# GpSimd instead of VectorE for eleven subtractions in each of two feed forwards

## The chip, the cores and the metric

The kernel is one program on one core of a Trainium2 chip. The metric is the device time of one execution in microseconds (us); less is better. The core has a matmul engine (TensorE, called PE in the profile, with its weight loads in a row of their own, PEld), three engines for elementwise work (VectorE or DVE, ScalarE or ACT, GpSimd or POOL) and a queue engine (SyncE or SP) that issues transfers. Each engine works through its own list of instructions in order and waits on semaphores for the others.

## The reference

The reference is one block of a transformer with 512 tokens of width 1024, all in float32:

```python
x = x + 0.5 * swiglu(rmsnorm(x, ffn1_norm), ffn1_w_gate, ffn1_w_up, ffn1_w_down)
x = x + token_mixer(rmsnorm(x, mix_norm), ...)      # differential and dilated attention
x = x + 0.5 * swiglu(rmsnorm(x, ffn2_norm), ffn2_w_gate, ffn2_w_up, ffn2_w_down)
return rmsnorm(x, final_norm)
# GpSimd instead of VectorE for eleven subtractions in each of two feed forwards
```

The change lies in the two feed forwards (the lines with `swiglu`).

## The kernel before

**Products in three parts.** The matmuls take operands in a rounded float32 format (`F32R`). To keep precision each operand is split: a high part, which is a rounded copy that ScalarE makes (`A.copy`), and a low part, value minus high part, which until now VectorE makes. A product is then high*high, high*low, low*high: the three matmuls of `mm3` (L157 uses the weight's high part with the moving operand's high part, L158 the moving operand's low part, L159 the weight's low part).

**Layout.** The activations lie transposed: eight tiles `x[0]` to `x[7]` of 128 features by 512 tokens. A weight arrives by a transfer into `raw`, ScalarE casts it to `w` (L148, or L436 for the later units), and VectorE makes its low part (L149, or L440).

**The order of a feed forward** (`ffn`, suffix `a` for the first and `b` for the second). Of the 22 column blocks of the gate and up matrices the first ones are plain: block j multiplies all eight x tiles in two halves of four. The blocks before `n0` (5 in the first feed forward, 3 in the second) use the x tiles before the norm is known, and VectorE scales the result (L265, L268, L269). While blocks `n0-2` and `n0-1` run on TensorE, `normed_x` makes the normed tiles: VectorE writes `nx` (L280), ScalarE the high part `xh` (L282), and the low part `xl` is L283. Block `n0` is the first that reads `xh` and `xl`. After it come units of seven products (Strassen's scheme for a 2x2 split of the matrices): they need sums and differences of the normed tiles (`t_sums`, L300 and L303, which overwrite `nx`), of which `t_casts` makes high parts (`tx`, L308) and `t_rests` low parts (`tt`: L317 for three of the four pairs of tiles, L320 for the fourth). In `t_rests(p, i)`, i = 0 gives the terms t1 and t3, i = 1 the terms t4 and t2, which the units read later.

**Sums of weights.** A unit also needs sums of weight blocks. SP loads one block into `s1` and `s3` (L378) and a transfer issued by POOL adds the second one (L379). These transfers are nearly all that POOL does.

**What sets the order.** Up to block `n0` the order on VectorE, ScalarE, SP and POOL is chosen by the framework's scheduler, which weighs each instruction by its place in the source and when its inputs are due. From block `n0` on (`schedule`, with the table `FIRST` for the sums) it is the order in which the source emits them, by due times written in nanoseconds. TensorE's order is always that of the source.

Of the kernel before, what the change touches and what calls it, by code (L numbers as in the profile page):

```python
# [14 lines left out]
F32 = mybir.dt.float32  # L15
# [3 lines left out]
ALU = mybir.AluOpType  # L19
# [63 lines left out]
def tile_macaron(ctx: ExitStack, tc, xs, xT, wf, wgu1, wst1, wd1, wdg1, wqk, wv, wo, wgu2, wst2, wd2,  # L83
                 wdg2, lams, relb, onehot, addc, out):
    nc = tc.nc
    V, A, G, T = nc.vector, nc.scalar, nc.gpsimd, nc.tensor
# [10 lines left out]
    def slot(i, nm, dt=F32):  # L97
        return sl.tile([P, S], dt, tag=f"slot{i}", name=nm)


    def flat(a):
        return a.rearrange("p (b a) -> p b a", b=2)

    def evens(a):
        return a.rearrange("p (a b) -> p b a", b=2)
# [7 lines left out]
    def side(a, i):  # L113
        return a.rearrange("p (b h a) -> p h b a", b=2, h=2)[:, i]
# [6 lines left out]
    xh = [cp.tile([P, S], F32R, tag=f"xh{k}", name=f"xh{k}") for k in range(KD)]  # L121
    xl = [cp.tile([P, S], F32R, tag=f"xl{k}", name=f"xl{k}") for k in range(KD)]
# [38 lines left out]
    def gain(norm, k):  # L161
        return sm[:, norm * KD + k:norm * KD + k + 1]
# [70 lines left out]
    def ffn(wgu, wst, wd, wdg, n0, n1, norm, early, res, nm, hooks, ended, first=None,  # L233
# [13 lines left out]
        nx, th, tl, held_parts = [], [], [], {}  # L247
# [27 lines left out]
        def normed_x(p):  # L275

            for k in (2 * p, 2 * p + 1):
                n = slot(8 + k, f"nx{nm}{k}")
                nx.append(n)
                V.scalar_tensor_tensor(flat(n[:]), evens(x[k]), gain(norm, k), evens(res["bc"][:]),  # L280
                                       op0=ALU.mult, op1=ALU.mult)
                A.copy(xh[k][:], n[:])  # L282
                V.tensor_tensor(xl[k][:], n[:], xh[k][:].bitcast(F32), op=ALU.subtract)  # L283

        def t_places():
            rows = [tp.tile([P, 5 * HS], F32R, tag=f"pr{p % 2}", name=f"tt{nm}{p}")
# [26 lines left out]
        def t_rests(p, i):  # L313
            t = nx[2 * p + i]
            if p < 3:
                c = slice(i * S, (i + 1) * S)
                V.tensor_tensor(tl[p][:, c], t[:], th[p][:, c].bitcast(F32), op=ALU.subtract)  # L317
            else:
                for q in range(2):
                    V.tensor_tensor(flat(tl[p][:, i * S + q * HS:i * S + (q + 1) * HS]),  # L320
                                    side(t[:], q),
                                    flat(th[p][2 * i + q]).bitcast(F32), op=ALU.subtract)
# [340 lines left out]
        def schedule():  # L663
# [43 lines left out]
            for i, (f, *v) in enumerate(FIRST):  # L707
                f = {"sums": t_sums, "casts": t_casts, "rests": t_rests, "part": lambda j, i: held_parts[n0 + j][i]()}[f]
                at(*v[:2], f, *v[2:])

        j0 = 0
        if first is not None:
            j0 = 2
            due += first

        prepare = {(n0 - 2 + p // 2, 1 + p % 2 * 4): (normed_x, p) for p in range(4)}

        def prepared(j, k):
# [7 lines left out]
        for j in range(j0, n1):  # L726
# [12 lines left out]
            for hf in range(2):  # L739
# [4 lines left out]
                for kk in range(4):  # L744
                    k = hf * 4 + kk
# [34 lines left out]
    with tc.manual_schedule(engines={mybir.EngineType.DVE, mybir.EngineType.Activation}):  # L780
        for t in range(4):
            raw = wp.tile([P, 1024], F32, tag="raw", name=f"raw_f{t}")
            h, l = w_place()
            for kk in range(2):
                k = 2 * t + kk
# [708 lines left out]
    for i, m in enumerate((WO + 1, WO + 3)):  # L1494
        a11, a12, a21, a22 = [wo[m + j // 2][:, j % 2 * 512:j % 2 * 512 + 512] for j in range(4)]
        for j, n, parts in ((0, "s3", (a11, a21)), (1, "s2", (a21, a22, a11)),
                            (2, "s1", (a21, a22)), (3, "s4", (a21, a22, a11, a12))):
            t = sums[m, n] = slot((32, 8)[i] + j, f"{n}wo{m}")
# [151 lines left out]
    for i, (m, (o, _, _)) in enumerate(seq):  # L1650
        if i > 3:
            t = max(start[i // 2 * 2 - 4] if i > 5 else 5.2, start[i] - 4.1)
# [4 lines left out]
        if o in ("a22", "s4"):  # L1657
            k, t = m + (o == "a22"), start[i + 1]
# [4 lines left out]
    with tc.manual_schedule(engines={mybir.EngineType.DVE, mybir.EngineType.Activation}):  # L1663
        while evs:
            e = min(evs, key=lambda e: e[:2])
# [210 lines left out]
```

## Time and profile before

| what | value |
| --- | --- |
| median of 3 runs | 896.49 us (896.14 to 896.87) |
| the profiled execution | 896.77 us, span in the trace 895.0 us |
| TensorE busy | 879.5 us of the span, 98% |
| VectorE busy | 766.7 us, 86%, 1603 instructions |
| ScalarE busy | 559.6 us, 63% |
| GpSimd busy | 111.6 us, 12%, 140 instructions |
| granted TensorE clock | 0.995 |

A row of a timeline reads: start in us, length in us, engine, line and operation, output<-inputs, shapes; in brackets the idle time of the engine before it and what ended that. A row of a group reads: line, engine, operation, count | busy us, mean ns of one | idle us before them. A recorded length is from the start to the end of one instruction; on VectorE neighbours overlap a little, so what an instruction costs its engine is the distance from one start to the next. The time of the profiled execution is the span and 1.8 us around it.

### The profile page before, as it was taken

What the parts mean: (1) busy time and instruction counts of PE and PEld (TensorE: products, weight loads), DVE (VectorE), ACT (ScalarE), POOL (GpSimd) and SP (SyncE); (2) the same over time, 40 slices, a digit from 0 to 9 for tenths busy, and PEclk for the clock granted to TensorE, in tenths of its full rate; (3) what the DMA queues carried; (4) which work ended last, traced back from release to release, by engine and by line L of the source; (5) the groups of instructions that cost most, each with busy time, mean ns of one, the idle gap of its engine ahead of it and who ended that gap; (6) DMA issues with size and microseconds to landing.
All of it is one profiled execution on the core that took longest, in us unless ns stands there. A gap on an engine that the chain in (4) does not pass through costs nothing.

```text
span 895.0 us, 17681 instructions
## 1 busy us (share of the span) xinstructions
PE 879.5 (98%) x6561; PEld 835.5 (93%) x6561; DVE 766.7 (86%) x1603; ACT 559.6 (63%) x1152; POOL 111.6 (12%) x140
## 2 busy tenths in 40 slices
PE   9999999999999999999999999999999999999996
PEld 7879999999999999998989889889999999999995
DVE  7799998787998995688998859999899778799897
ACT  7457775455776673666766858557677454667563
POOL 0001200112203100001010220001110111220100
PEclk9999999999999999999999999999999999999998
DMA  7447756678857843345365674646884857985842
GB/s 262 138 136 167 181 144 179 153 192 210 208 148 209 224 137 95 118 118 157 104 173 157 172 146 118 176 134 161 188 199 116 200 166 177 235 213 124 202 130 94
DMA packets 66374, 146.86 MB, mean 164 GB/s; under 512 B 7680, under 2 KB 9984, under 8 KB 66288
## 3 DMA queue, kind: packets, MB, share of 16 engines
q1 hardware_dynamic: 48672, 113.29, 39.2%
q0 software_dynamic: 17616, 32.45, 22.3%
q8 instruction: 51, 0.84, 0.4%
q14 instruction: 35, 0.29, 0.1%
HBM read 137.28 MB, written 2.14 MB: 156 GB/s over the span
## 4 chain that ended last, share of the span: by engine, by line
PE 74%; DVE 16%; ACT 5%; issue 3%; DMA 2%; SPq 0%; POOL 0%; DVEq 0%; ACTq 0%; POOLq 0%
DVE w L939 1%; DVE pr L1222 1%; PE po L1260 1%; DVE w L440 1%; PE pdb L157 1%; PE pdb L158 1%; PE pdb L159 1%; PE pda L158 1%; PE pda L157 1%; PE pda L159 1%; PE pxub L159 1%; PE pwgb L157 1%; PE pyub L159 1%; PE pwub L159 1%; PE pygb L159 1%
## 5 line engine op out<-in xcount | busy, mean ns | idle before, releaser
L1225 ACT ACTIVATE pr<-pr,small 128x128 f32<-128x128 f32 (+3 forms) x64 | 35.7, 559 | 30.3 <-DVE small L1222 30.0
L436 ACT CAST w<-s2b 128x512 fp32r<-128x512 f32 x52 | 32.6, 626 | 22.5 <-DVE s2b L418 21.8
L436 ACT CAST w<-s2a 128x512 fp32r<-128x512 f32 x48 | 29.9, 624 | 22.6 <-DVE s2a L418 18.9
L440 DVE TENSOR_TENSOR w<-s2b,w 128x512 fp32r<-128x512 f32 x52 | 36.0, 693 | 1.2 <-ACT w L436 1.1
L1222 DVE CUSTOM_DVE_ANT_0 pr<-sc,strip 128x128 f32<-128x128 f32 (+3 forms) x64 | 29.7, 487 | 8.1 <-PE sc L1221 8.0
L1005 PE MATMUL pv<-w,xh 128*128 128x256 f32 x128 | 35.7, 279 | 0.0
L1007 PE MATMUL pv<-w,xh 128*128 128x256 f32 x128 | 35.1, 274 | 0.0
L1006 PE MATMUL pv<-w,xl 128*128 128x256 f32 x128 | 35.1, 274 | 0.0
L440 DVE TENSOR_TENSOR w<-s2a,w 128x512 fp32r<-128x512 f32 x48 | 33.1, 690 | 0.8 <-ACT w L436 0.6
L939 DVE TENSOR_TENSOR w<-raw_qk,w 128x512 fp32r<-128x512 f32 x32 | 21.7, 688 | 5.3 <-ACT w L935 5.2
L157 PE MATMUL pq<-xh,w 128*128 128x512 f32 x64 | 26.0, 407 | 0.0
L157 PE MATMUL pk<-xh,w 128*128 128x512 f32 x64 | 24.3, 380 | 0.6 <-DVE ob L1285 0.6
L1006 PEld LDWEIGHTS pv<-w,xl 128*128 128x128 f32 x128 | 24.5, 191 | 0.1
L1005 PEld LDWEIGHTS pv<-w,xh 128*128 128x128 f32 x128 | 24.5, 191 | 0.1
L1007 PEld LDWEIGHTS pv<-w,xh 128*128 128x128 f32 x128 | 24.5, 191 | 0.0
L158 PE MATMUL pk<-xl,w 128*128 128x512 f32 x64 | 24.3, 379 | 0.0
L159 PE MATMUL pk<-xh,w 128*128 128x512 f32 x64 | 24.3, 379 | 0.0
L159 PE MATMUL pq<-xh,w 128*128 128x512 f32 x64 | 24.3, 379 | 0.0
L158 PE MATMUL pq<-xl,w 128*128 128x512 f32 x64 | 24.3, 379 | 0.0
L935 ACT CAST w<-raw_qk 128x512 fp32r<-128x512 f32 x32 | 19.3, 617 | 6.7 <-PE pv L1006 3.0
L1260 PEld LDWEIGHTS po<-v,ptb 128*128 128x128 f32 x160 | 21.5, 191 | 1.8 <-ACT ptb L1249 0.8
L1260 PE MATMUL po<-v,ptb 128*128 128x128 f32 (+1 forms) x160 | 22.1, 273 | 0.2 <-ACT ptb L1249 0.2
(841 smaller groups left out, 4135.1 us busy)
## 6 DMA issues: line engine op xcount, KB each, us to landing
raw_qk<-wqk_dram SPq DMA_DIRECT2D x16, 512.0 KB, 4.0
raw0bg<-wst_dram SPq DMA_DIRECT2D x9, 512.0 KB, 5.4
raw0bu<-wst_dram SPq DMA_DIRECT2D x9, 512.0 KB, 5.9
raw_gua<-wgu_dram SPq DMA_DIRECT2D x8, 512.0 KB, 3.4
raw0ag<-wst_dram SPq DMA_DIRECT2D x8, 512.0 KB, 5.2
raw0au<-wst_dram SPq DMA_DIRECT2D x8, 512.0 KB, 5.2
raw0ad<-wdg_dram SPq DMA_DIRECT2D x8, 512.0 KB, 6.0
strip<-bias_rows SPq DMA_DIRECT2D x16, 256.0 KB, 5.2
```

What stands on the lines that cost most here:

```text
L157: T.matmul(po, wh, mh, start=first, stop=False, skip_group_check=on)
L158: T.matmul(po, wh, ml, start=False, stop=False, skip_group_check=on)
L159: T.matmul(po, wl, mh, start=False, stop=last, skip_group_check=on)
L436: A.copy(made[t][0], source(t))
L440: V.tensor_tensor(l, source(t), h.bitcast(F32), op=ALU.subtract)
L939: V.tensor_tensor(l[:, c:c + 512], raw[:, c:c + 512], h[:, c:c + 512].bitcast(F32), op=ALU.subtract)
L1005: T.matmul(po, xh[k][:, xs], mh_, start=k == 0, stop=False)
L1006: T.matmul(po, xl[k][:, xs], mh_, start=False, stop=False)
L1007: T.matmul(po, xh[k][:, xs], ml_, start=False, stop=k == KD - 1)
L1222: V.tensor_tensor_reduce(out=o, in0=a, in1=b, op0=ALU.add, op1=ALU.min, scale=1.0, scalar=3.0e38, accum_out=st["mx"][:, m, i:i + 1])
L1225: A.activation(pi, pi, AF.Exp, scale=-1.0, bias=st["mx"][:, m, i:i + 1], accum_out=st["ls"][:, m, i:i + 1])
L1260: T.matmul(st["po3"][:, i, d0:d0 + dn], st["ptb", m, i][:, k * P:(k + 1) * P], vk, start=k == 0, stop=k == i)
```

## The change

Eleven subtractions of a feed forward are written for GpSimd in place of VectorE: the eight of `normed_x` (the low parts `xl`) and, in `t_rests`, those with i = 1 for the three pairs p < 3. Those with i = 0 and the fourth pair stay on VectorE. Both feed forwards call the same function, so 22 instructions move.

```diff
@@ normed_x
                 A.copy(xh[k][:], n[:])
-                V.tensor_tensor(xl[k][:], n[:], xh[k][:].bitcast(F32), op=ALU.subtract)
+                G.tensor_tensor(xl[k][:], n[:], xh[k][:].bitcast(F32), op=ALU.subtract)
@@ t_rests
             if p < 3:
                 c = slice(i * S, (i + 1) * S)
-                V.tensor_tensor(tl[p][:, c], t[:], th[p][:, c].bitcast(F32), op=ALU.subtract)
+                e = G if i else V
+                e.tensor_tensor(tl[p][:, c], t[:], th[p][:, c].bitcast(F32), op=ALU.subtract)
```

The added line moves all later line numbers by one (L317 becomes L318, L379 becomes L380, L440 becomes L441).

**GpSimd, first feed forward.** Its list in the changed kernel, from the second transfer of the first weight sums on (the tiles carry a running number behind their name; `xl_86` to `xl_93` are the eight low parts, `nxa` and `xh` their inputs; the rows of `xl_88` to `xl_91` read like their neighbours and are left out):

```order
L380 DMA s3ag_574<-wst_dram 128x512
L283 TENSOR_TENSOR xl_86<-nxa_457,xh_78 128x512
L283 TENSOR_TENSOR xl_87<-nxa_461,xh_79 128x512
L283 TENSOR_TENSOR xl_92<-nxa_583,xh_84 128x512
L283 TENSOR_TENSOR xl_93<-nxa_587,xh_85 128x512
L380 DMA s1au_652<-wst_dram 128x512
L380 DMA s3au_655<-wst_dram 128x512
L380 DMA s1ag_733<-wst_dram 128x512
L380 DMA s3ag_736<-wst_dram 128x512
L318 TENSOR_TENSOR tta_635<-nxa_461,txa 128x512
L318 TENSOR_TENSOR tta_636<-nxa_497,txa 128x512
L318 TENSOR_TENSOR tta_637<-nxa_545,txa 128x512
```

Before, the transfers stood there alone; now the eight subtractions stand ahead of those of the second unit (`s1au_652`), and the three others ahead of `s1au_865`. The second feed forward has the same pattern.

**VectorE, blocks 3 and 4 of the first feed forward.** Before, where `raw_gua_0_525` and `raw_gua_1_561` are the weights of the two halves of block 4:

```order
L280 SCALAR_TENSOR_TENSOR nxa_497<-x_99,x_104,rbc_n_379 128x512
L283 TENSOR_TENSOR xl_87<-nxa_461,xh_79 128x512
L283 TENSOR_TENSOR xl_88<-nxa_493,xh_80 128x512
L283 TENSOR_TENSOR xl_89<-nxa_497,xh_81 128x512
L149 TENSOR_TENSOR w<-raw_gua_0_525,w 128x1024
L280 SCALAR_TENSOR_TENSOR nxa_541<-x_100,x_104,rbc_n_379 128x512
L265 TENSOR_TENSOR t1a_513<-pga_439,rbc_n_379 128x512
L268 TENSOR_TENSOR t2a_516<-pua_440,rbc_n_379 128x512
L280 SCALAR_TENSOR_TENSOR nxa_545<-x_101,x_104,rbc_n_379 128x512
```

and now:

```order
L280 SCALAR_TENSOR_TENSOR nxa_497<-x_99,x_104,rbc_n_379 128x512
L149 TENSOR_TENSOR w<-raw_gua_0_525,w 128x1024
L280 SCALAR_TENSOR_TENSOR nxa_541<-x_100,x_104,rbc_n_379 128x512
L280 SCALAR_TENSOR_TENSOR nxa_545<-x_101,x_104,rbc_n_379 128x512
L149 TENSOR_TENSOR w<-raw_gua_1_561,w 128x1024
L265 TENSOR_TENSOR t1a_513<-pga_439,rbc_n_379 128x512
L280 SCALAR_TENSOR_TENSOR nxa_583<-x_102,x_104,rbc_n_379 128x512
L268 TENSOR_TENSOR t2a_516<-pua_440,rbc_n_379 128x512
```

The low part of the first half's weight follows the third `nxa` directly, and that of the second half has moved ahead of the scaling of block 3's result (L265 to L269). Further on, the scaling of block 4's result has moved behind the first sums.

**VectorE, the first unit of seven products.** Before:

```order
L440 TENSOR_TENSOR w<-s3ag_574,w 128x512
L317 TENSOR_TENSOR tta_635<-nxa_461,txa 128x512
L317 TENSOR_TENSOR tta_636<-nxa_497,txa 128x512
L440 TENSOR_TENSOR w<-s3au_655,w 128x512
L317 TENSOR_TENSOR tta_637<-nxa_545,txa 128x512
L418 TENSOR_TENSOR s2a_786<-s1au_652,raw0au 128x512
```

and now:

```order
L441 TENSOR_TENSOR w<-s3ag_574,w 128x512
L441 TENSOR_TENSOR w<-s3au_655,w 128x512
L419 TENSOR_TENSOR s2a_786<-s1au_652,raw0au 128x512
```

Only the three subtractions have left; nothing else has moved there. TensorE's list and SP's are the same as before, and ScalarE has the same instructions with some casts of `xh` moved ahead of a weight cast.

## The prediction

> **What bounds the kernel now.** The page's first rows give TensorE 98% of the span. So time can only be won where TensorE waits. I read its waits in the two stretches that the change touches, 28 to 100 us and 560 to 650 us; each list has one row (line waited at, what ended the wait, total us, times, longest).
>
> ```profile
> PE 879.5 (98%) x6561; PEld 835.5 (93%) x6561; DVE 766.7 (86%) x1603; ACT 559.6 (63%) x1152; POOL 111.6 (12%) x140
> PE pga L159 <- DVE w L149: 1.6, 2, 1.0
> PE pgb L159 <- DVE w L149: 0.2, 1, 0.2
> ```
>
> Both feed forwards wait for the low part of a plain block's weight, which VectorE makes late. The table by stretches gives the sums: length, then busy time (instructions) of PE, PEld, DVE, ACT, POOL, the granted clock, the DMA share and GB/s.
>
> ```profile
> 36.00:62.00 26.00, 24.37 (x112) 20.73 (x111) 25.96 (x38) 14.50 (x20) 0.00 (x0) 1.00 0.22 72
> 62.00:85.00 23.00, 23.00 (x163) 21.69 (x162) 23.00 (x49) 16.93 (x35) 5.28 (x6) 1.00 0.78 179
> 578.00:596.00 18.00, 17.77 (x83) 15.24 (x82) 18.00 (x26) 11.79 (x16) 0.00 (x0) 1.00 0.16 57
> 596.00:606.00 10.00, 10.00 (x48) 8.77 (x47) 10.00 (x24) 6.61 (x13) 3.96 (x5) 1.00 0.95 285
> ```
>
> TensorE idles 26.00 - 24.37 = 1.63 us in the first feed forward and 18.00 - 17.77 = 0.23 us in the second, and not at all behind that. VectorE is free for 0.04 us in the first of the four stretches and not at all in the others. It is thus the second bound, and in these stages whatever VectorE gains or loses arrives at TensorE as soon as VectorE's lead there is used up. The lead is the third thing to read. In the first unit of seven products the tightest place is the low part of `s2` of the up half (VectorE, L440) against the first matmul that reads it (L159):
>
> ```profile
> 80.59 0.77 DVE L440 TENSOR_TENSOR w<-s2a,w 128x512 fp32r<-128x512 f32 x1
> 82.18 0.28 PE L159 MATMUL pxua<-txa,w 128*128 128x256 f32 x1
> 615.47 0.68 DVE L440 TENSOR_TENSOR w<-s2b,w 128x512 fp32r<-128x512 f32 x1
> 616.25 0.33 PE L159 MATMUL pxub<-txb,w 128*128 128x256 f32 x1
> ```
>
> Lead: 82.18 - 81.36 = 0.82 us in the first feed forward, 616.25 - 616.15 = 0.10 us in the second. All eleven moved instructions lie ahead of this place in VectorE's list, so it collects their whole effect.
>
> **What VectorE is rid of.** Neighbours start 0.60 us apart, though each lasts longer:
>
> ```profile
> 43.23 0.72 DVE L269 TENSOR_TENSOR t1a<-t2a,t1a 128x512 f32<-128x512 f32 x1
> 43.83 0.73 DVE L283 TENSOR_TENSOR xl<-nxa,xh 128x512 fp32r<-128x512 f32 x1
> 44.43 0.97 DVE L280 SCALAR_TENSOR_TENSOR nxa<-x,x,rbc_n 128x512 f32<-128x512 f32 x1
> 77.78 0.77 DVE L317 TENSOR_TENSOR tta<-nxa,txa 128x512 fp32r<-128x512 f32 x1
> 78.38 0.77 DVE L418 TENSOR_TENSOR s2a<-s1au,raw0au 128x512 f32<-128x512 f32 x1
> ```
>
> L283 and L317 both cost 0.60 us, and 11 x 0.60 = 6.6 us per feed forward. The new order helps beyond that: the two weight low parts that TensorE waited for move forward.
>
> ```profile
> 39.40 1.10 ACT L148 CAST w<-raw_gua 128x1024 fp32r<-128x1024 f32 x1
> 44.79 1.05 ACT L148 CAST w<-raw_gua 128x1024 fp32r<-128x1024 f32 x1
> 49.39 1.35 DVE L149 TENSOR_TENSOR w<-raw_gua,w 128x1024 fp32r<-128x1024 f32 x1
> 50.80 0.48 PE L159 MATMUL pga<-eha,w 128*128 128x512 f32 x1 [0.62 <-DVE w L149]
> 55.81 1.39 DVE L149 TENSOR_TENSOR w<-raw_gua,w 128x1024 fp32r<-128x1024 f32 x1
> 57.25 0.48 PE L159 MATMUL pga<-eha,w 128*128 128x512 f32 x1 [1.01 <-DVE w L149]
> ```
>
> Their high parts were ready at 40.50 and 45.84, long before; only the queue on VectorE held the low parts back. Left alone, the change ends both waits and the one of the second feed forward: at best -1.63 - 0.23 = -1.86 us. Nothing more is to be had there, since TensorE has no other gap.
>
> **What GpSimd takes on.** The trace has no GpSimd instruction with two input tensors; the nearest rows are these (count | busy us, mean ns of one):
>
> ```profile
> masks.py:199 POOL TENSOR_SCALAR_AFFINE_SELECT ident<-ident 128x128 f32<-128x128 f32 x1 | 0.3, 289 | 0.0
> L1867 POOL MEMSET const-float32-1.0<- 128x1 f32 x1 | 0.1, 99 | 0.0
> ```
>
> 99 ns is the price of starting; (289 - 99)/127 = 1.50 ns is that of a column read and written. For 512 columns with one input: 99 + 511 x 1.50 = 865 ns. With two inputs it is at most twice per column, 1.63 us. I take 1.1 us, nearer the lower end, because the select also decides for each element. The duration alone does no harm. The low parts are first read here, and the last of them:
>
> ```profile
> 62.32 0.38 PE L158 MATMUL pga<-xl,w 128*128 128x512 f32 x1
> 72.03 0.38 PE L158 MATMUL pua<-xl,w 128*128 128x512 f32 x1
> 596.39 0.38 PE L158 MATMUL pgb<-xlb,w 128*128 128x512 f32 x1
> 58.85 0.62 ACT L282 CAST xh<-nxa 128x512 fp32r<-128x512 f32 x1 [0.20 <-DVE nxa L280]
> 593.64 0.62 ACT L282 CAST xh<-nxb 128x512 fp32r<-128x512 f32 x1 [0.20 <-DVE nxb L280]
> ```
>
> The last high part was there at 59.5 and 594.3, and comes earlier now. Eight subtractions of 1.1 us fill 8.8 us of a stretch of some 20 us in which GpSimd did nothing; even at 1.63 us the last `xl` ends near 61 (59.5 + 1.63), eleven us before it is read. The three `tt` have their last input at 72.1 and are needed from 80.7 on:
>
> ```profile
> 71.51 0.62 ACT L308 CAST txa<-nxa 128x512 fp32r<-128x512 f32 x1
> 80.73 0.28 PE L158 MATMUL pxga<-tta,w 128*128 128x256 f32 x1
> 71.63 1.10 POOL L379 DMA_DIRECT2D s1au<-wst_dram  x1
> 97.35 0.63 ACT L436 CAST w<-s3au 128x512 fp32r<-128x512 f32 x1
> ```
>
> They also push the transfer for `s1au`, issued at 71.63, to about 76, and what it and its partner bring is read at 97. That part costs nothing.
>
> **The price that decides** is what a GpSimd subtraction costs VectorE while it runs; call it c. Both engines read the same memory, VectorE has no free time, and nearly all its instructions there read two tensors of SBUF as well. The trace shows no such overlap: the select above ran before VectorE's first instruction, and what runs on POOL later are issues of transfers. So c lies between 0 (the engines do not disturb each other) and 1.63 us (VectorE stands still while GpSimd works). I take one-at-a-time use: 1.1 us less the 0.1 us by which VectorE's neighbours overlap (0.72 recorded, 0.60 apart), c = 1.0. One of the eleven meets the pair L265 and L268, which read a result bank and one tensor, and I let it go free. VectorE's net delay at the tight place is then D = 10c - 6.6 = +3.4 us.
>
> TensorE moves by D less the lead, and by no less than the gaps it can close: first feed forward 3.4 - 0.82 = +2.6 us, second 3.4 - 0.10 = +3.3 us. The sum is +5.9 us on 896.77, so 902.7 in the profiled execution; the median stands 0.28 below that execution, which gives **902.4 us**. The general form is max(-1.63, D - 0.82) + max(-0.23, D - 0.10): c = 0.71 gives zero, c = 0.865 (the price of one input, undiminished) 899.9 or 899.7 as a median, c = 1.63 would give 18.5 us more.
>
> The Trainium skill bears on c directly. Its page "SBUF — State Buffer", section "Who interferes with whom", states that a VectorE instruction with two SBUF inputs contends with a GpSimd instruction that reads SBUF, and that the loser blocks for a whole instruction; no run here shows it yet. Its "GPSIMD Engine Reference", section "Performance versus the Vector engine", has 4497 ns for a two-input add of 2048 columns, a quarter of which is 1.12 us; by it c = 1.02 and the sum would be +6.3 us.
>
> **GpSimd's own queue.** The subtractions stand ahead of the transfers that add the second weight block:
>
> ```profile
> 599.77 0.87 POOL L379 DMA_DIRECT2D s1bu<-wst_dram  x1 [29.32 <-PE pgb L159]
> 600.38 1.15 POOL L379 DMA_DIRECT2D s3bu<-wst_dram  x1
> s3bu<-wst_dram POOLq DMA_DIRECT2D x2, 256.0 KB, 7.5
> 608.71 0.62 ACT L436 CAST w<-s3bu 128x512 fp32r<-128x512 f32 x1
> ```
>
> In the second feed forward the sum `s3bu` lands about 600.38 + 7.5 = 607.9, and its cast starts at 608.71: 0.8 us to spare. The eight subtractions must be through before 599.77. With the last input there by 594.3 they are, by 4 us at c = 0; in the forecast VectorE delivers it 7 x 1.0 - 8 x 0.60 = 2.2 us later, at 596.5, and one more subtraction with its wait for VectorE's instruction ends near 598.5. I take nothing for it.
>
> **Rivals.**
>
> *No interference.* c is under 0.58, GpSimd works for free, D is under -0.8, and only the gaps close: 896.49 - 1.86 = 894.6. For it: no row shows a conflict, and VectorE's spacing stays at 0.60 us in 70 to 84 us while POOL issues transfers. Against it: those issues read no tensor.
>
> *Break-even.* The engines share by turns in smaller steps, so that c is 0.58 to 0.80: VectorE loses about what it gets rid of, and the total is -1.8 to +1.9 us, about 896.5.
>
> *GpSimd starves instead.* VectorE keeps its pace and the subtractions run only beside L265 and L268. By 62.3 three or so of eight are done; then VectorE stands before L300, which overwrites what GpSimd has still to read, for about five subtractions, 5.5 us, and later for three, 3.3 us. D is 8.8 - 6.6 = +2.2, the sum +1.4 + 2.1 = +3.5 us: 900.0. It is slower like the forecast, but by waits at L300 in place of long instructions.
>
> *GpSimd's queue holds up the transfers.* If its subtractions in the second feed forward end after 599.77 + 0.8, `s3bu` is late for its cast, and TensorE waits; three subtractions behind would be 3 x 1.1 - 0.8 = +2.5 us, 899.0 without any conflict with VectorE. Against it are the 4 us to spare.
>
> That the change does not do what it says is out: the lists of the two engines show the instructions moved.
>
> **How the numbers follow.** One-at-a-time use with c above 0.80, the forecast: 0.46. Starved GpSimd: 0.06. Held transfers: 0.05. Break-even: 0.18. No interference: 0.25. Between 0.2% faster and 0.2% slower (1.8 us), about what a measurement of this kernel can tell from no change, lies the break-even case and nearly half of the case without interference, since its 1.86 us is just the bound: same 0.18 + 0.10 = 0.28, faster 0.15, slower 0.57. The likeliest case's own range is 899.7 (c = 0.865) to 907.6 (c = 1.26: D = 6.0, and +5.2 + 5.9 = +11.1 on the median). The range must hold the other side too: from 894.4, a little under the free case, to 907.6, beyond which I leave one in ten.
>
> **What would show it.** Right: VectorE's instructions in 41 to 60 us and at the three `tt` grow from 0.7 towards 1.7 us wherever GpSimd works, GpSimd's own are 1.0 to 1.3 us, the waits at L149 of the first feed forward are smaller than 1.63 in total, and new waits of TensorE for L441 appear at the first units of both feed forwards, 2 to 4 us each. Wrong: VectorE keeps 0.60 us between starts beside a GpSimd subtraction and shows idle time before the first unit. The starved case would show GpSimd spans of several us and VectorE idle before L300. What would upset the number most is c: each 0.1 us moves the result by 2 us.

## The result, and the profile after

The changed kernel takes 906.22 us (median of 5 runs, 903.46 to 906.78) where the kernel before takes 896.23 us beside it (5 runs, 896.07 to 896.87). The ratio is 1.0105 with a 95% interval of 1.0094 to 1.0116: slower by 9.4 us (8.4 to 10.4; the ratio weighs all runs, and the two medians alone stand 10.0 us apart). Two slow runs, one of the kernel before (2350.66 us) and one of the fills with zeros further down (1297.67 us), are in no ratio. The forecast was 902.4 us, with a range up to 907.6; the direction was right and the size was short by 3.8 us.

The profiled execution of the changed kernel is the fastest of its five: 903.46 us, span 901.3 us against 895.0 us before, +6.3 us. The other four are 2.2 to 3.3 us longer, at a mean granted clock of 0.993 to 0.995 where this one had 0.997. A profile of one at the median comes with the last experiment. The engine row of the page reads:

```profile
PE 879.7 (98%) x6561; PEld 835.3 (93%) x6561; DVE 770.8 (86%) x1581; ACT 558.3 (62%) x1152; POOL 156.0 (17%) x162
```

VectorE has 22 instructions fewer (1581 for 1603) and is busy 4.1 us *longer* (770.8 for 766.7). GpSimd is busy 44.4 us longer for the 22 instructions it has taken on, 2.0 us each. TensorE's work is the same, and in this execution its granted clock was 1.00 up to the last 6 us, so the time lies in its waits. Its list of waits in the changed kernel, 28 to 100 us and then 560 to 660 us (total us, times, longest):

```profile
PE pzga L159 <- DVE w L441: 1.4, 1, 1.4
PE pga L159 <- DVE w L149: 1.2, 2, 0.8
PE pwua L159 <- DVE w L441: 0.3, 1, 0.3
PE pwga L159 <- DVE w L441: 0.2, 1, 0.2
PE pgb L159 <- DVE w L149: 1.6, 1, 1.6
PE pzgb L159 <- DVE w L441: 1.5, 1, 1.5
PE pwgb L159 <- DVE w L441: 0.9, 1, 0.9
PE pwub L159 <- DVE w L441: 0.3, 1, 0.3
```

Before there were 1.6 and 0.2 us, both at L149. Now it is 3.1 and 4.3 us, and all of it ends with VectorE: the plain weight's low part (L149) is still late, and the low parts of the first unit's weights (L441) are late as well.

**Where VectorE lost it.** The timeline of the changed kernel at the three `tt` of the first feed forward (start, length, engine, line, output<-inputs):

```profile
74.28 5.12 POOL L318 TENSOR_TENSOR tta<-nxa,txa 128x512 fp32r<-128x512 f32 x3
75.39 1.19 DVE L441 TENSOR_TENSOR w<-raw0au,w 128x512 fp32r<-128x512 f32 x1
76.50 1.76 DVE L419 TENSOR_TENSOR s2a<-s1ag,raw0ag 128x512 f32<-128x512 f32 x1
78.19 1.76 DVE L441 TENSOR_TENSOR w<-s3ag,w 128x512 fp32r<-128x512 f32 x1
79.87 0.68 DVE L441 TENSOR_TENSOR w<-s3au,w 128x512 fp32r<-128x512 f32 x1
80.00 0.38 PE L159 MATMUL pzga<-txa,w 128*128 128x256 f32 x1 [1.38 <-DVE w L441]
```

While GpSimd works on its three subtractions, three VectorE instructions of the 0.68 us kind take 1.19, 1.76 and 1.76 us; the next one, after GpSimd is done, takes 0.68 again. A full collision thus costs VectorE 1.76 - 0.68 = **1.08 us**. The matmul waits for the last of the stretched ones (78.19 + 1.76 = 79.95). The same happens to the eight `xl` of the first feed forward, with one exception, the first:

```profile
40.76 1.49 POOL L283 TENSOR_TENSOR xl<-nxa,xh 128x512 fp32r<-128x512 f32 x1 [17.05 <-ACT xh L282]
41.02 0.67 DVE L265 TENSOR_TENSOR t1a<-pga,rbc_n 128x512 f32<-128x512 f32 x1
45.25 6.04 POOL L283 TENSOR_TENSOR xl<-nxa,xh 128x512 fp32r<-128x512 f32 x3 [3.00 <-ACT xh L282]
47.84 2.31 DVE L149 TENSOR_TENSOR w<-raw_gua,w 128x1024 fp32r<-128x1024 f32 x1
52.74 1.22 DVE L149 TENSOR_TENSOR w<-raw_gua,w 128x1024 fp32r<-128x1024 f32 x1
52.75 7.80 POOL L283 TENSOR_TENSOR xl<-nxa,xh 128x512 fp32r<-128x512 f32 x4 [1.45 <-ACT xh L282]
59.33 2.31 DVE L149 TENSOR_TENSOR w<-raw_gua,w 128x1024 fp32r<-128x1024 f32 x1
```

The first subtraction ran beside L265 and L268, which read a result bank and one tensor, and they kept their 0.67 us. Its recorded 1.49 us holds a part of L269 (40.43 to 41.09), which reads two tensors of SBUF and had started first. A subtraction that nothing held up comes in the second feed forward, while VectorE stands idle: it lasted **1.26 us**.

```profile
593.80 1.26 POOL L283 TENSOR_TENSOR xlb<-nxb,xhb 128x512 fp32r<-128x512 f32 x1
```

The weight's low part took 2.31 us where a subtraction was running when its turn came, and 1.22 us where it had started first (52.74); then the subtraction, recorded from 52.75 on, was the one that lasted longer, 2.38 us. From the distances between the starts, the seven later subtractions cost VectorE 6.1 us and the three `tt` 2.7 us, together 8.8 us for ten collisions, 0.88 each. Two of the three at the `tt` were full ones. The shorter stalls (0.4 to 0.5 us) came right behind L265, L268 or L272, which read a result bank and beside which a part of the subtraction could be done.

**The second feed forward went another way.** Its eight subtractions begin like this:

```profile
582.20 14.10 POOL L283 TENSOR_TENSOR xlb<-nxb,xhb 128x512 fp32r<-128x512 f32 x4 [9.43 <-ACT xhb L282]
591.68 0.67 DVE L269 TENSOR_TENSOR t1b<-t2b,t1b 128x512 f32<-128x512 f32 x1
592.29 0.41 DVE L300 TENSOR_TENSOR nxb<-nxb 128x256 f32<-128x256 f32 x1
595.10 1.48 DVE L300 TENSOR_TENSOR nxb<-nxb 128x256 f32<-128x256 f32 x1 [2.41 <-POOL xlb L283]
```

Four subtractions took 14.1 us: GpSimd got hardly a turn, and VectorE kept its pace up to 592. Then L300 had to overwrite an `nx` that GpSimd had still to read, VectorE stood for 2.41 us, and after that five instructions in a row were stretched, short ones too (1.48 for 0.41 us). By the distances between starts the whole comes to 10.6 us here: 2.5 us at the wait, 5.3 us for the stretched instructions up to 603 us, 2.8 us at the three `tt`. So the forecast's case (turn by turn) and its rival (GpSimd starves) are both in one trace.

**The two halves of the span.** One VectorE instruction at the start of the second feed forward, L229, serves as a mark (before, then after):

```profile
576.45 0.69 DVE L229 COPY rbc_n<-bc_n 128x512 f32<-128x512 f32 x1
```

```profile
578.18 0.69 DVE L229 COPY rbc_n<-bc_n 128x512 f32<-128x512 f32 x1
```

It comes 1.73 us later; the remaining 6.3 - 1.7 = 4.6 us come behind it, with the second feed forward. The experiments below give the same two numbers ("up to the mark", "behind it").

### The profile page after: what moved, and what is told of

The parts are those of the page before. It is cut to its first block, busy times and chain, and to the rows that moved or that the text cites. A ratio compares the mean times of both kernels' runs of the same rounds, so it can differ in the third digit from the quotient of the medians.

```text
span 901.3 us, 17690 instructions
## 1 busy us (share of the span) xinstructions
PE 879.7 (98%) x6561; PEld 835.3 (93%) x6561; DVE 770.8 (86%) x1581; ACT 558.3 (62%) x1152; POOL 156.0 (17%) x162
## 4 chain that ended last, share of the span: by engine, by line
PE 69%; DVE 18%; ACT 5%; issue 5%; DMA 2%; POOL 1%; SPq 0%; DVEq 0%; ACTq 0%; POOLq 0%
DVE w L441 2%; DVE w L940 1%; PE po L1261 1%; DVE pr L1223 1%; PE pdb L159 1%; PE pdb L157 1%; PE pdb L158 1%; DVE w L149 1%; PE pda L157 1%; PE pda L158 1%; PE pda L159 1%; PE pyub L157 1%; PE pxgb L157 1%; PE pxub L157 1%; PE pygb L157 1%
## 5 line engine op out<-in xcount | busy, mean ns | idle before, releaser
L441 DVE TENSOR_TENSOR w<-s2b,w 128x512 fp32r<-128x512 f32 x52 | 35.7, 686 | 1.2 <-ACT w L437 1.0
L441 DVE TENSOR_TENSOR w<-s2a,w 128x512 fp32r<-128x512 f32 x48 | 33.1, 690 | 0.8 <-ACT w L437 0.6
L1317 POOL DMA_DIRECT2D mx<-mh x4 | 2.3, 582 | 146.6 <-ACT mh L1301 146.6
L380 POOL DMA_DIRECT2D s1bd<-wdg_dram x8 | 7.0, 869 | 100.3 <-DMA s3bd<-wdg_dram 34.7
```

Source lines behind the costliest of these rows:

```text
L441: V.tensor_tensor(l, source(t), h.bitcast(F32), op=ALU.subtract)
```

## The experiments

The theory: while a GpSimd instruction reads SBUF, a VectorE instruction with two SBUF inputs stands still, at about 1 us per subtraction, and that eats more than the 6.6 us per feed forward that VectorE is rid of. The rivals: it is the new order of VectorE's list; it is GpSimd's slowness (what it makes is late); it is the writing, not the reading. The edits of the first four experiments are to the changed kernel, those of the next three to the kernel before. All times stand against the kernel before on the same chip (896.26 us for the first four, 896.13 us for the others).

### Only the eight low parts on GpSimd

```diff
-                e = G if i else V
+                e = V
```

> The eight low parts of the normed tiles stay on GpSimd, the three of the sums go back to VectorE. Theory (one engine at a time reads the shared memory path; each meeting costs VectorE about 1.08 us, as the 1.76 instead of 0.68 us of L419 show): VectorE saves 8 x 0.60 = 4.8 us and pays 7 x 1.08 = 7.6 us per feed forward, D = +2.8; first feed forward 2.8 - 0.82 = +2.0 us, second +2.7 us, together +4.7 us. Rival (only the three of the sums hurt, because they meet the tightest stretch; the eight have ten us of slack): -1.9 to 0 us.

Measured: 900.93 us, ratio 1.0053 (1.0039 to 1.0068), +4.7 us. In its profile the mark comes 1.2 us later and the part behind it takes 3.1 us more. So the `xl` alone cost half of what the whole change costs. The sum is the theory's, but not its parts (+2.0 and +2.7 us).

### Only the three others on GpSimd

```diff
-                G.tensor_tensor(xl[k][:], n[:], xh[k][:].bitcast(F32), op=ALU.subtract)
+                V.tensor_tensor(xl[k][:], n[:], xh[k][:].bitcast(F32), op=ALU.subtract)
```

> The three low parts of the sums stay on GpSimd, the eight of the normed tiles go back to VectorE. Theory (one at a time): VectorE saves 1.8 us and pays 3 x 1.08 = 3.2 us, D = +1.4 per feed forward; +0.6 and +1.3 us, together +2.0 us. Rival (the eight do all of the harm, by filling GpSimd's queue ahead of the transfers): 0 us.

Measured: 898.38 us, ratio 1.0027 (1.0015 to 1.0039), +2.4 us; +0.2 us up to the mark and +1.3 us behind it in the profiled execution. The new waits of TensorE in the two stretches:

```profile
PE pzga L159 <- DVE w L441: 0.5, 1, 0.5
PE pzgb L159 <- DVE w L441: 1.3, 1, 1.3
```

The old waits at L149 stand unchanged (1.6 and 0.2 us), and one new wait per feed forward has come, at the matmul that the changed kernel waits at too. It is not the place that the prediction took for the tightest one. In the kernel before, the same weight's low part and the same matmul:

```profile
75.37 0.78 DVE L440 TENSOR_TENSOR w<-s3ag,w 128x512 fp32r<-128x512 f32 x1
78.16 0.28 PE L159 MATMUL pzga<-txa,w 128*128 128x256 f32 x1
610.25 0.68 DVE L440 TENSOR_TENSOR w<-s3bg,w 128x512 fp32r<-128x512 f32 x1
612.23 0.28 PE L159 MATMUL pzgb<-txb,w 128*128 128x256 f32 x1
```

The lead here is larger, 78.16 - 76.15 = 2.0 us and 612.23 - 610.93 = 1.3 us. But VectorE's order is L440 for `s3ag` first and the three moved L317 behind it, while the three collisions fall ahead of it. So this matmul gets the whole cost, 2.8 and 2.7 us by the starts, and none of the 3 x 0.60 us saved. It comes 2.8 - 2.0 = 0.8 us later in the first feed forward and 2.7 - 1.3 = 1.4 us in the second, together +2.2 us, near the +2.4 measured.

By their medians the two parts give 4.7 + 2.4 = 7.1 of 9.4 us. In the profiled executions they give 4.3 + 1.5 = 5.8 of 6.3 us, so there is little that only both together cost. A typical execution of the changed kernel, shown at the end of the experiments, has two things that these profiles have not: longer stalls at the `tt` and a stretch of lower clock.

### GpSimd writes and reads nothing

Each of the eleven becomes a fill with zeros, so the low parts are left out of the products; order and number of instructions on VectorE stay.

```diff
-                G.tensor_tensor(xl[k][:], n[:], xh[k][:].bitcast(F32), op=ALU.subtract)
+                G.memset(xl[k][:].bitcast(F32), 0.0)
...
+                if i:
+                    G.memset(tl[p][:, c].bitcast(F32), 0.0)
```

> GpSimd writes zeros into the eleven low parts and reads nothing; VectorE does none of them. This leaves the low parts out of the computation. Theory (the harm is the reading): VectorE is rid of 6.6 us and pays nothing, all waits for L149 close, -1.9 us. Rival (the harm is the new order of VectorE and ScalarE, which is the same here): as much slower as the changed kernel, +6 to +10 us.

Measured: 895.27 us, ratio 0.9987 (0.9977 to 0.9996), -1.2 us; the interval (-2.1 to -0.4 us) holds the -1.9 us of the theory. TensorE has no wait left in the two stretches. The profiled execution is the fastest one (893.91 us), with 2.5 us gained up to the mark and 0.7 us behind it. The timeline at the `tt`:

```profile
68.96 1.89 POOL L319 MEMSET tta<- 128x512 f32 x3
70.50 0.69 DVE L272 TENSOR_TENSOR t1a<-pua,t1a 128x512 f32<-128x512 f32 x1 [1.48 <-ACT t1a L271]
```

No VectorE instruction is stretched, and VectorE even has 1.48 us to spare. The fills of `xl` went to the start of the program, since they have no input, and those at the `tt` ran almost wholly while VectorE was idle. So this run says nothing of what a fill does to a VectorE instruction beside it. What it does show: with VectorE's list in the same order as in the changed kernel, and without GpSimd's subtractions beside it, the kernel is not slower. The order is not the cause.

### GpSimd reads one tensor in place of two

The eleven become plain copies of `nx` (or `t`), so the low parts are not computed.

```diff
-                G.tensor_tensor(xl[k][:], n[:], xh[k][:].bitcast(F32), op=ALU.subtract)
+                G.tensor_copy(xl[k][:], n[:])
...
+                if i:
+                    G.tensor_copy(tl[p][:, c], t[:])
```

> GpSimd copies the normed tile or the sum into the low part's place: one input instead of two, so the low parts are not computed. Theory (one at a time, price by GpSimd's own duration): a copy of 512 columns takes about 0.87 us by the select's 1.50 ns a column, so c is about 0.8 and D = 8.0 - 6.6 = +1.4 us; together +0.6 + 1.3 = +1.9 us. Rival (only two-input instructions of GpSimd disturb): -1.9 us.

Measured: 893.71 us, ratio 0.9975 (0.9966 to 0.9984), -2.2 us; 2.7 us are gained up to the mark and 0.8 us behind it. One copy that nothing held up, beside L268, and the `tt`:

```profile
54.44 0.62 POOL L283 CAST xl<-nxa 128x512 fp32r<-128x512 f32 x1 [0.81 <-DVE nxa L280]
69.37 5.38 POOL L319 CAST tta<-nxa 128x512 fp32r<-128x512 f32 x3
72.58 0.67 DVE L444 TENSOR_TENSOR w<-s3ag,w 128x512 fp32r<-128x512 f32 x1
73.18 1.09 DVE L444 TENSOR_TENSOR w<-s3au,w 128x512 fp32r<-128x512 f32 x1
```

Neither statement held as it stood. The copies do disturb VectorE, which the rival denied (its -1.9 us came near for another reason), but at 1.09 - 0.67 = **0.42 us** each, half of what the theory had put in. Ten of those would be 4.2 us, under the 6.6 us saved, so VectorE gains and TensorE's waits close in both stretches. What failed in the theory is the length, 0.87 us taken from the select; the copy itself lasts 0.62 us. So both prices are the GpSimd instruction's own length less 0.2 us: 1.26 and 1.08 us for the subtraction, 0.62 and 0.42 us for the copy. That fits one engine at a time. Two pairs are no law, though, and as a copy reads half as much and is half as long, this run does not tell which of the two sets the price. The number of columns written does not, since it is the same in both. Some copies are recorded at up to 9.27 us, starved behind VectorE, and it harms nothing, since they are early enough.

### The subtractions on both engines

The kernel before, with VectorE's work unchanged; GpSimd does the same eleven once more into a buffer that nobody reads. This adds work and takes none away.

```diff
+                V.tensor_tensor(xl[k][:], n[:], xh[k][:].bitcast(F32), op=ALU.subtract)
+                G.tensor_tensor(sq[:], n[:], xh[k][:].bitcast(F32), op=ALU.subtract)
```

> VectorE keeps all its work as before; GpSimd makes the eleven subtractions a second time, into a tile that is free then, and nobody reads them. Theory (each meeting costs VectorE 1.08 us): D = 10 x 1.08 = 10.8 us per feed forward, 10.8 - 0.82 and 10.8 - 0.10, together about +20 us; less where GpSimd does not get its turn. Rival (the harm is that TensorE or VectorE waits for low parts that GpSimd makes late): 0 us, since nobody waits for these.

Measured: 913.89 us, ratio 1.0196 (1.0183 to 1.021), +17.6 us. Nothing waits for GpSimd's values here, yet the kernel loses nearly twice what the change lost: +7.4 us up to the mark, +8.8 us behind it. A part of it is again the overwriting at L300 (here L301):

```profile
DVE nxa L301 <- POOL sq L284: 5.1, 2, 2.5
```

Here no gain stands against GpSimd's subtractions, so the loss is theirs: by VectorE's stretched instructions, by these 5.1 us at L301, and by what follows from TensorE's long waits. In two stretches around such waits (the rows are in the last section) the granted clock was one half, which took up to 5 us of the 17.6. So the difference to the changed kernel, 17.6 - 9.4 = 8.2 us, does not measure the 2 x 6.6 = 13.2 us that VectorE is rid of there.

### The new order alone

The kernel before, all eleven on VectorE, with the eight `xl` written further down in the source, so that the weights' low parts go first.

```diff
+        def low_x(p):
+            for k in (2 * p, 2 * p + 1):
+                V.tensor_tensor(xl[k][:], nx[k][:], xh[k][:].bitcast(F32), op=ALU.subtract)
...
+            for p, kk in enumerate((3, 5, 6, 7)):
+                if (j, k) == (n0 - 1, kk):
+                    low_x(p)
```

> All eleven subtractions stay on VectorE, but the eight low parts of the normed tiles are written later in the source, so that the weights' low parts go ahead of them, as in the changed kernel. GpSimd does nothing new. Theory (VectorE is the second bound, its lead at the first unit is 0.82 and 0.10 us): D = 0, so the gain ends at -0.82 - 0.10 = -0.9 us although all gaps of 1.86 us could close. Rival (the order alone was worth the whole 1.86 us): -1.9 us.

Measured: 895.95 us, ratio 0.9998 (0.9989 to 1.0008), -0.2 us: no difference that can be told. Its profiled execution has a span of 894.1 us, 0.9 us less than before, and one wait of 0.9 us at L149 in place of two. But the trace before is itself 0.6 us above the median beside this run (896.77 and 896.13 us), so the trace shows no gain either that can be told. The interval (-1.0 to +0.7 us) holds the -0.9 us of the theory as well as nothing at all; it leaves out the rival's -1.9 us.

### One subtraction per feed forward on GpSimd

The order of the last experiment, and one `xl` of the eight on GpSimd: the first one in the first feed forward (beside L265 and L268), the seventh in the second.

```diff
+        gp = (0,) if n0 == EARLY[0] else (6,)
+                if k in gp:
+                    G.tensor_tensor(xl[k][:], n[:], xh[k][:].bitcast(F32), op=ALU.subtract)
```

> As the order alone, but one low part of each feed forward goes to GpSimd: the first tile's in the first feed forward, the seventh tile's in the second, which should fall beside L265 and L268 (one SBUF input each). Theory: the one of the first feed forward is free, D = -0.6 there, -1.4 us; the one of the second costs at most 0.5 us, D = -0.1, -0.2 us; together -1.6 us. If any GpSimd subtraction costs VectorE its full 1.08 us: D = +0.5 in both, -0.3 + 0.4 = about 0 us.

Measured: 894.71 us (11 runs, 894.25 to 895.14), ratio 0.9981 (0.9973 to 0.999), -1.7 us. It is faster than both kernels, and 1.2 us faster than the order alone. In the first feed forward the subtraction lies as meant, and the VectorE instruction beside it (L266 is L265 of the changed kernel) keeps its length:

```profile
40.67 1.45 POOL L285 TENSOR_TENSOR xl<-nxa,xh 128x512 fp32r<-128x512 f32 x1 [16.00 <-ACT xh L283]
40.89 0.68 DVE L266 TENSOR_TENSOR t1a<-pga,rbc_n 128x512 f32<-128x512 f32 x1
588.00 9.30 POOL L285 TENSOR_TENSOR xl<-nxb,xh 128x512 fp32r<-128x512 f32 x1 [19.61 <-ACT xh L283]
```

In the second it missed its place: the pair had run at 585.12 and 585.72, before its input was there, and it took 9.30 us, up to 597.3. VectorE was not held up by it, and its next pair ran at 595.92 and 596.52, near its end. So the second half of this result is luck of the starved kind and not the design. The kernel gains 1.9 us up to the mark and 0.6 us behind it.

### The changed kernel once more

> The changed kernel once more, for a second trace. Theory (who gets its turn first is decided anew in each execution): the time lies between 903 and 907 us, and the lengths of GpSimd's single instructions differ from those of the first trace, while its stretched VectorE neighbours again last 1.0 to 1.1 us longer. If the meeting were fixed by the order alone, the two traces would agree instruction by instruction.

Measured: 906.63 us (2 runs), ratio 1.0116 (1.0098 to 1.0135). This time the profiled execution is a typical one: 906.62 us, span 904.5 us, +9.5 us. Its eight `xl` in the first feed forward lie as in the first profile (6.08 us for three, 7.78 us for four). The `tt` do not:

```profile
75.03 4.05 POOL L318 TENSOR_TENSOR tta<-nxa,txa 128x512 fp32r<-128x512 f32 x3
75.53 4.11 DVE L441 TENSOR_TENSOR w<-raw0au,w 128x512 fp32r<-128x512 f32 x1
79.56 0.68 DVE L419 TENSOR_TENSOR s2a<-s1ag,raw0ag 128x512 f32<-128x512 f32 x1
79.69 0.58 PE L159 MATMUL pwua<-xh,w 128*128 128x256 f32 x1 [1.59 <-DVE w L441]
615.54 4.41 POOL L318 TENSOR_TENSOR ttb<-nxb,txb 128x512 fp32r<-128x512 f32 x3
616.24 4.27 DVE L441 TENSOR_TENSOR w<-raw0bu,w 128x512 fp32r<-128x512 f32 x1
620.57 0.38 PE L159 MATMUL pwub<-xhb,w 128*128 128x256 f32 x1 [2.45 <-DVE w L441]
```

Here one VectorE instruction is held for all three subtractions: 4.11 us for 0.68, from start to start 4.03 - 0.60 = 3.4 us in the first feed forward and 3.6 us in the second, where the other profile had 2.7 and 2.8. The mark comes 4.2 us late, and 9.5 - 4.2 = 5.3 us come behind it. TensorE's clock has a part in the first number. The table by stretches of this execution (length, then busy time and instructions of PE, PEld, DVE, ACT, POOL, granted clock, DMA share, GB/s), and the same three microseconds of the kernel before:

```profile
80.00:83.00 3.00, 3.00 (x16) 3.00 (x16) 3.00 (x7) 2.34 (x5) 0.82 (x1) 0.51 0.79 111
83.00:86.00 3.00, 3.00 (x29) 3.00 (x28) 2.95 (x6) 1.85 (x5) 0.00 (x0) 1.00 0.35 64
```

```profile
80.00:83.00 3.00, 3.00 (x29) 3.00 (x29) 3.00 (x8) 2.82 (x7) 0.00 (x0) 1.00 0.03 3
```

After the wait of 1.59 us (the one that ends at 79.69) the granted clock was 0.51 for 3 us, and 16 matmuls went through where 29 did before: 3.00 x (1 - 0.51) = about 1.5 us lost. The first profile of the changed kernel has no such stretch, which may be a part of why it was the fastest of its five; the other three left no trace.

## Why the prediction was right, and where it was short

**The bound (right) and the gap (too small).** TensorE bounds the kernel and VectorE stands right behind it; nearly every wait of TensorE that the changed kernel and the experiments have in the two feed forwards ends with a VectorE instruction. But 1.86 us as all that can be won was too little. The run with one input has no wait left there, and matmul by matmul (the traces have the same 6561 in the same order) TensorE gains 2.2 us on the kernel before from 45 to 60 us and 0.5 us from 590 to 596 us, 2.7 us in all. The median's -2.2 us (-3.0 to -1.4) would allow either. The gaps were read from TensorE's idle time, in which the matmul ahead of a wait still counts as busy. By the starts it is more. The kernel before, at the two waits of its first feed forward:

```profile
49.80 0.38 PE L158 MATMUL pga<-ela,w 128*128 128x512 f32 x1
50.80 0.48 PE L159 MATMUL pga<-eha,w 128*128 128x512 f32 x1 [0.62 <-DVE w L149]
51.12 0.38 PE L157 MATMUL pua<-eha,w 128*128 128x512 f32 x1
```

Neighbours start 0.22 us apart; from 49.80 to 51.12 two steps took 1.32 us, 0.88 us too long, where the bracket says 0.62: 0.26 us more than its bracket for this wait.

**What VectorE is rid of (right, but not at every place).** 0.60 us per instruction held. That the moved L149 would end TensorE's waits there was only half right. Of the two in the first feed forward the second (1.01 us) is gone and the first fell from 0.62 to 0.31 us, since L149 was stretched to 2.31 us (at 47.84); a new one of 0.85 us came at 61.69, behind the L149 stretched at 59.33. The order alone has one of 0.88 us at the same matmul, so that this one is not GpSimd's doing alone.

**What GpSimd takes (near).** Taken as 1.1 us with bounds 0.865 to 1.63; it is 1.26 us where nothing held it up. That its own lateness does no harm held for the `tt`. It failed for the `xl` of the second feed forward: L300 waited 2.41 us for them in the first profile (and 1.2 us in the second). The step looked at who reads what GpSimd makes, and not at who overwrites what it still has to read; that stood only in a rival, at 0.06. The queued transfer for `s1bu` went out at 602.27 in place of 599.77, and no wait of TensorE for it shows.

**The price c (right in kind, near in size by some luck).** The step said one-at-a-time use, 1.0 us; a full collision is 1.08 us. Both terms of it were short, the length (1.1 for 1.26 us) and the part that costs nothing (0.1 for 0.2 us), and the two errors cancel. The instruction beside a result-bank reader is free, as assumed (0.67 us beside the first subtraction). The Trainium skill, page "SBUF — State Buffer", section "Who interferes with whom", says that a VectorE instruction with two SBUF inputs contends with a GpSimd instruction that reads SBUF, over a pair of ports that it calls "an exclusive lock"; the traces agree (1.76 us for 0.68, 0.67 us beside a result bank). The Trainium skill's "GPSIMD Engine Reference", section "Performance versus the Vector engine", has 4497 ns for a two-input add of 2048 columns, of which a quarter, an estimate, is 1.12 us; the trace has 1.26 us, and that decides.

**The sum (the place was wrong, and a term was missing).** The general form, delay D less VectorE's lead, holds. The term 10c was taken as 10.0 us per feed forward and measured 8.8 and 10.6 us in the first profile, 9.5 and 11.2 us in the repeat: 8.8 us where the engines take turns, 9.5 us where VectorE is held for three subtractions in a row, 10.6 and 11.2 us where GpSimd starves first and VectorE must wait for it at L300. What failed is the sentence that the place at `s2` "collects their whole effect". TensorE waits earlier, at the matmul of the weights' sum `s3` (80.00 us, and its like in the second feed forward). There all ten collisions have happened, but only the eight `xl` have been saved, 4.8 us and not 6.6; the lead is 2.0 and 1.3 us. With these terms the first profile is 8.8 - 4.8 - 2.0 = +2.0 us and 10.6 - 4.8 - 1.3 = +4.5 us, together +6.5 us, against +1.7 up to the mark and +4.6 behind it, +6.3 in all. The forecast had +2.6 and +3.3; at its own place the measured costs would give +1.4 and +3.9 us, 1 us too little.

In the repeat TensorE waits at a weight earlier still (L441 of `raw0`), where the kernel before has leads of 1.9 us (76.82 - 74.94) and 1.2 us (610.89 - 609.73): 9.5 - 4.8 - 1.9 = +2.8 us, 1.5 us of lower clock, and 11.2 - 4.8 - 1.2 = +5.2 us, together +9.5 us, as measured. So the forecast's +5.9 us fell short of the typical execution by three terms: about 1.4 us by the place, 0.7 us by 10c, and 1.5 us by the granted clock after a long wait, which the prediction did not have.

**The signs.** Right: VectorE's instructions grow to 1.7 us, the waits at L149 of the first feed forward are smaller (1.2 us), and new waits for L441 come at the first units of both feed forwards. Those were foretold as 2 to 4 us each; the longest single ones are 1.4 and 1.5 us (1.6 and 2.5 us in the repeat), and all for L441 together 1.9 and 2.7 us (2.1 and 3.6 us). GpSimd's own instructions were foretold as 1.0 to 1.3 us; they are 1.26 us free of VectorE and 1.5 to 2.4 us where they take turns with it (those that starve much longer).

**The rivals.** No interference (894.6 us) and break-even fell: c is 1.08 us. Starved GpSimd was real in one half of the kernel, in addition to the forecast's case. Held transfers did not show.

What stays open: what decides who gets the next turn. The same subtraction took 1.5 to 2.4 us in turns, 4 to 11 us behind back-to-back VectorE instructions, or held one VectorE instruction for three in a row; the two profiles of one and the same kernel differ in it. That it is the reading, and not GpSimd's instruction as such, that stops VectorE is argued and not shown: no run has a fill beside a VectorE instruction with two SBUF inputs.

## What to carry to other kernels

An instruction handed from VectorE to GpSimd comes off VectorE's account only as far as GpSimd's instruction does not stop VectorE: here 0.60 us were taken off and up to 1.08 us put back, so that even free GpSimd time made the kernel slower. Before offloading, compare the two prices: two input tensors lost, one input tensor (0.42 us) gained, and beside VectorE instructions that read a result bank it was free. Here, where VectorE's own time is the second bound, a new order and one offload per feed forward (-1.7 us, in part by luck) did more than eleven (+9.4 us).

A delay of VectorE reaches TensorE at the first matmul whose lead it uses up. So the sum is to be made at each such matmul by itself: a cost counts there if it falls ahead of it in VectorE's order, and a saving only if it does too. The three `tt` cost 2.7 us ahead of the matmul that waited, and their 1.8 us of savings lay behind it.

## What the runs showed of the hardware that was not expected

- A price below one to one: the same 128x512 tile, copied by GpSimd, cost VectorE 0.42 us, and with a second input 1.08 us; in both cases that is the GpSimd instruction's own length, where nothing held it up (0.62 and 1.26 us), less 0.2 us.
- No fair turns: a GpSimd instruction of 1.26 us took 9.30 us, and in the run with the subtractions on both engines up to 10.7 us (at 52.42), behind VectorE instructions that follow each other without a gap, and elsewhere VectorE was held 4.11 us for three GpSimd instructions.
- The granted clock fell to one half for a few microseconds around the end of some long waits of TensorE. In the run with the subtractions on both engines, where waits of 1.96 and 2.44 us end at 74.30 and 77.33 and one of 5.49 us ends at 603.93:

```profile
77.00:81.00 4.00, 3.67 (x18) 3.67 (x19) 4.00 (x8) 3.41 (x8) 3.92 (x2) 0.57 0.83 137
603.00:611.00 8.00, 7.07 (x19) 5.72 (x20) 6.95 (x10) 2.02 (x3) 5.07 (x1) 0.57 0.56 183
```

A mean of 0.57 over 4 and 8 us is one half for 3.4 and 6.9 us. It does not follow each long wait: in the repeat of the changed kernel the clock stayed at 1.00 after the 2.45 us at 620.57, though it fell after the 1.59 us at 79.69. What else it takes was not tried.
